# Hybrid diffusion step on one core: modulation chunks beside the long convolution, made as TensorE products instead of sums on VectorE, ScalarE and GpSimd

## The chip, the cores and the metric

The kernel runs on one core of one Trainium2 chip. The metric is the device time of one execution in microseconds (us). Engines are named as in the profile: PE is TensorE (PEld its weight loads), DVE VectorE, ACT ScalarE, POOL GpSimd, SP the queue that issues the DMAs. PE writes only to PSUM, which has eight banks of 128 partitions x 512 fp32 numbers.

## What is computed

Four layers run one after the other over 128 context tokens and 1024 latent tokens of width 1024: a long (FFT) convolution, latent attention, a recurrent mixer, and a long convolution again. Each layer begins with a modulation whose shift, scale and gate come from a condition vector, one for the latents and one for the context:

```python
def _modulation(cond, w, b):
    m = jax.nn.silu(cond) @ w + b
    return jnp.split(m, 3, axis=-1)
...
    for i in range(DEPTH):
        sh_p, sc_p, g_p = _modulation(c_ctx[None, None, :], mod_w[i], mod_b[i])
        sh_s, sc_s, g_s = _modulation(c[:, None, :], mod_w[i], mod_b[i])
        hp = xp * (1.0 + sc_p) + sh_p
        hs = xs * (1.0 + sc_s) + sh_s
...
    vf = jnp.fft.rfft(v.astype(jnp.float32), n=2 * L, axis=1)
    kf = jnp.fft.rfft(filt, axis=0)
    y = jnp.fft.irfft(vf * kf[None], n=2 * L, axis=1)[:, :L].astype(h.dtype) + v * skip
    y = y * x0
    return (y * jax.nn.silu(z)) @ w_out
```

So for each layer two vectors of 1024 are multiplied into a matrix `mod_w[i]` of 1024 x 3072. The matrix is 12 MB in fp32 and is read once for both conditions.

## The kernel before

**Modulation.** The 3072 columns are cut into six parts of 512: parts 0 and 1 are the shift, 2 and 3 the scale, 4 and 5 the gate. `mod_part` makes one part in eight steps, one for each 128 rows of the matrix (k = 0 to 7). A step loads a 128 x 512 piece (`modw`, 256 KB, two buffers) by SP at L296. DVE multiplies it by the latents' condition and adds it to `macc0` (L299 for k = 0, L302 for the rest). ACT multiplies it by the context's condition into `mprod` (L304; L300 writes `macc1` itself for k = 0), which has one buffer, and POOL adds `mprod` to `macc1` (L305). After the eighth step PE adds up the 128 partitions: for shift and scale as eight products with a column of ones, each with 128 columns of `macc` as weights (L314); for the gate as one product for each condition with the ones as weights (L326), to which DVE adds the bias (L329).

**Where the parts run.** While layer i runs, it makes its own gate (parts 4 and 5) and the next layer's shift and scale (parts 0 to 3). The first layer of all has its own shift and scale made at the start by `mod_fast`, on PE (L355). So the first layer makes six parts beside its mixer and the last one two.

**The long convolution.** Layers 0 and 3 first make the filter's spectra (`ps_ft`, `ps_sp` on PE). Then the 1024 channels go through in four units of 256 (`conv_long`). A unit transposes its signal `vx` on PE (L1073) and ACT copies it to `xt` (L1075); DVE does a first butterfly stage into `su`. Nine residues then pass through a pipeline: ACT and POOL split the fp32 numbers in two (`sh` and `sl`, L267 and L268), PE multiplies (three products each, L262 to L264, into `ps_fw`), DVE multiplies by the filter (L1108), POOL adds (L1110, L1111), ACT and POOL split again (`zh`, `zl`), PE transforms back (`ps_iv`), ACT copies out (L1137). DVE's inverse butterflies (L722 to L799) end the unit and `yc` is stored. Between these, PE does the layer's dense projections (`ps_mm<-hh,wh`, 128 x 384 each), whose results ACT copies out and DVE filters with three taps (L1006) and multiplies (L1023) into the next unit's `vx`.

**What sets the order.** The program is written as generators that `weave` interleaves by given numbers of steps: in each unit the residues, the dense jobs and 12 steps of modulation. A scheduler then sets each engine's final order. On the chip each engine runs its own list in order and waits on semaphores, and SP issues its DMAs in order. The PSUM tiles take turns through the banks that `set_banks` gives to their kind:

```python
        self.set_banks(mm=(0, 1), tp_ax_fw_iv=(2, 3, 4, 5, 6, 7))
        for q in range(NU):
            xt, xp = blocks(q, keep)
            weave((conv_long(q, keep, wpool, xt, xp), LQ[q]), (part_gen(dense, steps[q + 1]), steps[q + 1]),
                  (part_gen(rest, 12 if q < NU - 1 else 99), 12))
...
            rest = chain_gens(*(p.mod_part(*x) for x in parts))
```

Of the kernel before, what the change touches and what calls it, by code (L numbers as in the profile page):

```python
# [10 lines left out]
F32 = mybir.dt.float32  # L11
# [3 lines left out]
ALU = mybir.AluOpType  # L15
# [5 lines left out]
P = 128  # L21
D = 1024
KC = D // P
# [141 lines left out]
def weave(*jobs):  # L165

    for _ in woven(*jobs):
        pass
# [29 lines left out]
def chain_gens(*gens):  # L198
    for g in gens:
        yield from g  # L200


def part_gen(gen, steps):

    for _ in range(steps):
        try:
            next(gen)
        except StopIteration:
            return
        yield  # L210
# [12 lines left out]
class Prog:  # L223
# [66 lines left out]
    def mod_part(self, i, part):  # L290

        nc = self.nc
        acc = [self.mp.tile([P, 512], F32, tag=f"macc{c}", name=f"macc{c}", bufs=1) for c in range(2)]
        for k in range(KC):
            w = self.mp.tile([P, 512], F32, tag="modw", name="modw", bufs=2)
            nc.sync.dma_start(w, self.A["mod_w"][i, k * P:(k + 1) * P, part * 512:(part + 1) * 512])  # L296
            s, sp = self.cond[:, 0, k:k + 1], self.cond[:, 1, k:k + 1]
            if k == 0:
                nc.vector.tensor_scalar(acc[0], w, s, None, op0=ALU.mult)  # L299
                nc.scalar.activation(acc[1], w, AF.Copy, scale=sp)  # L300
            else:
                nc.vector.scalar_tensor_tensor(acc[0], w, s, acc[0], op0=ALU.mult, op1=ALU.add)  # L302
                wp = self.mp.tile([P, 512], F32, tag="mprod", name="mprod", bufs=1)
                nc.scalar.activation(wp, w, AF.Copy, scale=sp)  # L304
                nc.gpsimd.tensor_tensor(acc[1], acc[1], wp, ALU.add)  # L305
            yield
        third, half = divmod(part, 2)
        if third < 2:
            if i not in self.hsc:
                self.hsc[i] = self.cp.tile([P, 2, 2, KC], F32, tag="hsc", name=f"hsc{i}", bufs=2)  # L310
            ps = self.psum("ax")
            for c in range(2):
                for j in range(4):
                    nc.tensor.matmul(ps[:, c * 4 + j:c * 4 + j + 1], acc[c][:, j * P:(j + 1) * P],  # L314
                                     self.ones[:, 0:1], start=True, stop=True)
            for c in range(2):
                nc.vector.tensor_tensor(self.hsc[i][:, c, third, half * 4:half * 4 + 4], ps[:, c * 4:c * 4 + 4],
                                        self.vec[:, i, third, half * 4:half * 4 + 4], ALU.add)
            if third == 1 and half == 1 and i > self.first:
                self.fold_mod(i)  # L320
        else:
            if i not in self.gate:
                self.gate[i] = self.dp.tile([2, D], F32, tag="gate", name=f"gate{i}", bufs=1)
            for c in range(2):
                ps = self.psum("ax")
                nc.tensor.matmul(ps[0:1], self.ones[:, 0:1], acc[c], start=True, stop=True)  # L326
                grow = self.mp.tile([1, 512], F32, tag="mprod", name="grow", bufs=1)
                nc.sync.dma_start(grow, self.A["mod_b"][i:i + 1, part * 512:(part + 1) * 512])
                nc.vector.tensor_tensor(grow, ps[0:1], grow, ALU.add)  # L329
                nc.sync.dma_start(self.gate[i][c:c + 1, half * 512:(half + 1) * 512], grow)  # L330

    def mod_fast(self, i):

        nc = self.nc
        self.hsc[i] = self.cp.tile([P, 2, 2, KC], F32, tag="hsc", name=f"hsc{i}", bufs=2)
        rows = {}

        def channels(part):
            third, half = divmod(part, 2)
            row = rows.pop(part)  # L340
            ps = self.psum("tp")
            for j in range(4):
                nc.tensor.transpose(ps[:, 2 * j:2 * j + 2], row[:, j * P:(j + 1) * P], self.ident[:2, :2])
            for c in range(2):
                nc.vector.tensor_tensor(self.hsc[i][:, c, third, half * 4:half * 4 + 4], ps[:, c:8:2],
                                        self.vec[:, i, third, half * 4:half * 4 + 4], ALU.add)

        for part in range(4):
            acc = self.psum("mm")[:2]
            for k in range(0, KC, 2):  # L350
                w = self.wp.tile([P, 2, 512], F32, tag="wl" if k % 4 else "wh", name="modw2")
                nc.sync.dma_start(w, self.A["mod_w"][i, k * P:(k + 2) * P, part * 512:(part + 1) * 512]
                                  .rearrange("(k p) n -> p k n", p=P))
                for c in range(2):
                    nc.tensor.matmul(acc, self.cond[:, :, k + c], w[:, c], start=k + c == 0, stop=k + c == KC - 1)  # L355
                if part and k == 2:
                    channels(part - 1)
                yield
            rows[part] = self.mp.tile([2, 512], F32, tag="mprod", name="mrow", bufs=1)
            nc.vector.tensor_copy(rows[part], acc)  # L360
        channels(3)
        self.fold_mod(i)
# [606 lines left out]
    def hyena(self, i, j, lead, rest):  # L969

        nc, A, tc = self.nc, self.A, self.tc
# [189 lines left out]
        with tc.tile_pool(name="hf", bufs=1, reuse_waits="tile") as fpool:  # L1161
# [10 lines left out]
                weave((begin(), 14), (part_gen(flt, FLT), FLT))  # L1172
                steps[0] -= NG
            weave((flt, FLX - (FLT + FLA if i == self.first else 0)), (part_gen(dense, steps[0]), steps[0]))
        self.set_banks(mm=(0, 1), tp_ax_fw_iv=(2, 3, 4, 5, 6, 7))
        keep = pools.enter_context(tc.tile_pool(name="hk", bufs=1, reuse_waits="tile"))
        work = ExitStack()
        wpool = work.enter_context(tc.tile_pool(name="hl", bufs=1, reuse_waits="tile"))
# [1079 lines left out]
def build(tc, A, O, layers=(0, 1, 2, 3)):  # L2258
    with ExitStack() as ctx:
        p = Prog(ctx, tc, A, O)  # L2260
        p.setup_cond()
        first, last = layers[0], layers[-1]
        p.first = first
        lead = p.first_h()
        for i in layers:
            j = i // 3
            parts = [(i, n) for n in (4, 5)] + [(i + 1, n) for n in range(4) if i != last]
            rest = chain_gens(*(p.mod_part(*x) for x in parts))
            if i in (0, 3):
                y = p.hyena(i, j, lead, rest)  # L2270
                w_out = A["hy_w_out"][j]
            else:
                weave(lead)
                y = (p.mla if i == 1 else p.rwkv)(i, rest)
                w_out = A["mla_w_out"] if i == 1 else A["rw_w_out"]
            lead = iter(())
            p.boundary(i, w_out, y, i == last)
# [61 lines left out]
```

## Time and profile before

| what | value |
|---|---|
| time, median of 3 runs | 4587.96 us (4586.16 to 4589.27) |
| the profiled execution: its own time, its span | 4590.18 us, 4588.4 us |
| mean granted TensorE clock | 0.925 |
| PE busy | 4061.0 us (89%) |
| DVE busy | 3504.3 us (76%) |
| ACT busy | 2392.5 us (52%) |
| POOL busy | 2360.3 us (51%) |

The profile is of one execution. Busy time counts an engine's own instructions, and the rest of the span it waits. The chain of work that ended last lies for 23% on PE, 5% on DVE, 3% on DMAs and 3% on ACT. The granted clock is 1.0 for 2.4 GHz and 0.5 for 1.2 GHz. An fp32 product appears as two records on PE, so 64 records of L355 are 32 products.

### The profile page before, as it was taken

How to read it: one execution, taken by the hardware profiler on the slowest of the kernel's cores; microseconds unless marked ns; L12 is line 12 of the kernel's file. 1: busy time of each engine (PE TensorE's matmuls, PEld its weight loads, DVE VectorE, ACT ScalarE, POOL GpSimd, SP SyncE). 2: the span in 40 equal slices, each digit the busy share in tenths (PEclk: the TensorE clock that was granted, in tenths of full speed). 3: DMA queues.
4: the chain of work that ended last, by engine and by line, in shares of the span. 5: the costliest groups of instructions: out<-in, count | busy, mean ns of one | idle time of the engine just before them, and what ended most of it. 6: DMA issues, size and time to landing. Idle time of an engine off the chain costs nothing. (4 is left out here: it accounts for less than half of the span.)

```text
span 4588.4 us, 83899 instructions
## 1 busy us (share of the span) xinstructions
PE 4061.0 (89%) x30888; PEld 3510.6 (77%) x30888; DVE 3504.3 (76%) x6147; ACT 2392.5 (52%) x5468; POOL 2360.3 (51%) x1902
## 2 busy tenths in 40 slices
PE   7988988889999999879979786999999889988988
PEld 4888888678777776658867575878888678878986
DVE  7777888655998999687587997677767668967877
ACT  5554433455666666453455553666666456543331
POOL 3655766253677877455555564333333233466550
PEclk8999999999999999989988797999999899999999
DMA  5755555643000000326635464222322424665455
GB/s 169 239 181 176 164 156 157 191 149 99 19 22 21 18 28 30 121 91 203 188 108 198 145 222 136 59 79 84 83 75 68 142 93 120 214 205 153 141 155 179
DMA packets 490982, 583.04 MB, mean 127 GB/s; under 512 B 59818, under 2 KB 378332, under 8 KB 489932
## 3 DMA queue, kind: packets, MB, share of 16 engines
q1 hardware_dynamic: 489068, 576.70, 40.7%
q8 instruction: 244, 4.00, 0.4%
q14 instruction: 166, 1.36, 0.1%
q10 hardware_dynamic: 1504, 0.98, 0.1%
HBM read 413.74 MB, written 161.37 MB: 125 GB/s over the span
## 5 line engine op out<-in xcount | busy, mean ns | idle before, releaser
L262 PE MATMUL ps_mm<-hh,wh 128*128 128x384 f32 x1728 | 597.0, 347 | 47.4 <-ACT hh L267 24.0
L263 PE MATMUL ps_mm<-hl,wh 128*128 128x384 f32 x1728 | 595.6, 345 | 2.8 <-DVE hl L268 1.8
L264 PE MATMUL ps_mm<-hh,wl 128*128 128x384 f32 x1728 | 594.5, 344 | 2.7 <-POOL wl L268 2.7
L1499 POOL TENSOR_TENSOR sm<-sm,pf 128x512 f32<-128x512 f32 x288 | 443.4, 1540 | 121.8 <-ACT pf L1492 48.8
L268 POOL TENSOR_TENSOR wl<-wraw,wh 128x512 fp32r<-128x512 f32 x212 | 331.5, 1581 | 187.4 <-ACT wh L267 175.3
L262 PEld LDWEIGHTS ps_mm<-hh,wh 128*128 128x128 f32 x1728 | 335.9, 195 | 55.5 <-ACT hh L267 25.1
L1497 DVE TENSOR_TENSOR wl<-pf,wh 128x512 fp32r<-128x512 f32 x288 | 352.8, 1235 | 6.6 <-ACT wh L1493 5.8
L263 PEld LDWEIGHTS ps_mm<-hl,wh 128*128 128x128 f32 x1728 | 336.2, 195 | 7.5 <-DVE hl L268 4.4
L264 PEld LDWEIGHTS ps_mm<-hh,wl 128*128 128x128 f32 x1728 | 336.0, 194 | 6.4 <-POOL wl L268 3.8
L305 POOL TENSOR_TENSOR macc<-macc,mprod 128x512 f32<-128x512 f32 x140 | 211.8, 1513 | 178.0 <-ACT mprod L304 155.4
L263 PE MATMUL ps_mm<-mx,wh 128*128 128x384 f32 x680 | 253.6, 373 | 37.9 <-DVE mx L1669 36.9
L262 PE MATMUL ps_mm<-mx,wh 128*128 128x384 f32 x680 | 255.9, 378 | 19.9 <-ACT mx L1668 6.1
L262 PE MATMUL ps_mm<-woh,hh 128*128 128x512 f32 x576 | 233.8, 407 | 37.0 <-ACT hh L267 34.6
L2144 POOL TENSOR_TENSOR tot<-SV,wcs 64x128 f32<-64x128 f32 x288 | 115.6, 405 | 267.9 <-DVE SV L2172 245.2
L264 PE MATMUL ps_mm<-mx,wl 128*128 128x384 f32 x680 | 247.0, 364 | 3.1 <-POOL wl L268 3.1
L1492 ACT ACTIVATE pf<-ps_st 128x512 f32<-128x512 f32 x288 | 172.3, 598 | 144.9 <-POOL sm L1499 53.3
L264 PE MATMUL ps_mm<-woh,hl 128*128 128x512 f32 x576 | 234.1, 406 | 3.7 <-DVE hl L268 3.7
L302 DVE SCALAR_TENSOR_TENSOR macc<-modw,cond,macc 128x512 f32<-128x512 f32 x140 | 156.5, 1118 | 103.3 <-DMA modw<-mod_w 102.4
L1437 DVE TENSOR_REDUCE mx<-ps_pj 128x1 f32<-128x512 f32 (+2 forms) x400 | 220.4, 575 | 17.2 <-PE ps_pj L1436 16.4
L263 PE MATMUL ps_mm<-wol,hh 128*128 128x512 f32 x576 | 231.8, 402 | 0.0
L304 ACT ACTIVATE mprod<-modw,cond 128x512 f32<-128x512 f32 x140 | 101.3, 723 | 205.5 <-POOL macc L305 108.6
L1493 ACT ACTIVATE wh<-ps_st 128x512 fp32r<-128x512 f32 x336 | 194.3, 578 | 0.0
(560 smaller groups left out, 13149.2 us busy)
## 6 DMA issues: line engine op xcount, KB each, us to landing
cst<-cst SPq DMA_DIRECT2D x175, 384.0 KB
modw<-mod_w SPq DMA_DIRECT2D x160, 256.0 KB
wraw<-hy_w_in SPq DMA_DIRECT2D x128, 256.0 KB
kd<-kt SPq DMA_DIRECT2D x72, 384.0 KB
kt<-kd SPq DMA_DIRECT2D x72, 384.0 KB
cst<-cst SPq DMA_DIRECT2D x41, 512.0 KB
ctd<-ct SPq DMA_DIRECT2D x24, 768.0 KB
bkd<-bk SPq DMA_DIRECT2D x24, 768.0 KB
```

The source lines that it names most:

```text
L262: mm(ps, lh, rh, start=start, stop=False)
L263: mm(ps, lh, rl, start=False, stop=False)
L264: mm(ps, ll, rh, start=False, stop=stop)
L268: (lo_eng or self.nc.gpsimd).tensor_tensor(lo, src, hi, ALU.subtract)
L302: nc.vector.scalar_tensor_tensor(acc[0], w, s, acc[0], op0=ALU.mult, op1=ALU.add)
L305: nc.gpsimd.tensor_tensor(acc[1], acc[1], wp, ALU.add)
L1437: nc.vector.tensor_reduce(mx[:, t, j:j + 1], ps, AX.X, ALU.max)
L1492: nc.scalar.activation(pf, s, AF.Exp, scale=scale)
L1493: nc.scalar.activation(ph, s, AF.Exp, scale=scale)
L1497: nc.vector.tensor_tensor(pl, pf, ph, ALU.subtract)
L1499: nc.gpsimd.tensor_tensor(sm, sm, pf, ALU.add)
L2144: g_.tensor_tensor(tot[h], SV[e][h, jsl], wc[h].unsqueeze(2).broadcast_to([64, 2, 64]), M)
```

## The change

In layers 0 and 3 the parts are made by a new generator `mod_rows`. Both conditions, as a 128 x 2 weight, are multiplied with each 128 x 512 piece on PE, and the eight products add up in one bank, in fp32. That bank (7) is taken from the group for transposes, residues and inverse, which is left with five. After the eighth product DVE copies the two rows out, PE transposes four pieces of 2 x 128, and DVE adds the bias for shift and scale; for the gate DVE adds the bias to the two rows and one DMA stores both. `mod_part` stays for layers 1 and 2.

```diff
+    def mod_rows(self, i, part):
+
+        nc, cols = self.nc, slice(part * 512, (part + 1) * 512)
+        acc = self.psum("md")[:2]
+        for k in range(KC):
+            w = self.mp.tile([P, 512], F32, tag="modw", name="modw", bufs=2)
+            nc.sync.dma_start(w, self.A["mod_w"][i, k * P:(k + 1) * P, cols])
+            nc.tensor.matmul(acc, self.cond[:, :, k], w, start=k == 0, stop=k == KC - 1)
+            yield
+        third, half = divmod(part, 2)
+        row = self.mp.tile([2, 512], F32, tag="mprod", name="mrow", bufs=1)
+        if third < 2:
...
+            nc.vector.tensor_copy(row, acc)
+            ps = self.psum("ax")
+            for j in range(4):
+                nc.tensor.transpose(ps[:, 2 * j:2 * j + 2], row[:, j * P:(j + 1) * P], self.ident[:2, :2])
+            for c in range(2):
+                nc.vector.tensor_tensor(self.hsc[i][:, c, third, half * 4:half * 4 + 4], ps[:, c:8:2],
+                                        self.vec[:, i, third, half * 4:half * 4 + 4], ALU.add)
...
+        else:
...
+            nc.sync.dma_start(row, self.A["mod_b"][i, cols].partition_broadcast(2))
+            nc.vector.tensor_tensor(row, acc, row, ALU.add)
+            nc.sync.dma_start(self.gate[i][:, half * 512:(half + 1) * 512], row)
...
-        self.set_banks(mm=(0, 1), tp_ax_fw_iv=(2, 3, 4, 5, 6, 7))
+        self.set_banks(mm=(0, 1), tp_ax_fw_iv=(2, 3, 4, 5, 6), md=(7,))
...
-            rest = chain_gens(*(p.mod_part(*x) for x in parts))
+            rest = chain_gens(*((p.mod_rows if i in (0, 3) else p.mod_part)(*x) for x in parts))
```

The added function moves all later lines by 30 (L1073 becomes L1103). In the new kernel L338 is the load of `modw`, L339 the product, L346 and L359 what DVE does with the two rows, L349 the transposes.

The scheduler's order changes with it. First PE in layer 0, where the first unit ends and the signal of the second is transposed (`ps_tp`). Before:

```order
L262 MATMUL ps_mm<-hh,wh 128x384
L263 MATMUL ps_mm<-hl,wh 128x384
L264 MATMUL ps_mm<-hh,wl 128x384
L1073 MATMUL ps_tp<-ident,vx 128x128 x13
L262 MATMUL ps_fw<-sh,cst 128x256
L263 MATMUL ps_fw<-sl,cst 128x256
```

and after the change:

```order
L262 MATMUL ps_mm<-hh,wh 128x384
L263 MATMUL ps_mm<-hl,wh 128x384
L264 MATMUL ps_mm<-hh,wl 128x384
L1103 MATMUL ps_tp<-ident,vx 128x128 x13
L339 MATMUL ps_md<-modw,cond 2x512 x2
L262 MATMUL ps_fw<-sh,cst 128x256
```

The products (`ps_md`) stand in PE's own list between its other work. Of the 48 in layer 0, six pairs follow one another directly and 36 stand alone; of the 16 in layer 3, three pairs and ten alone. From the last inverse product of the first unit to these 13 transposes the list has 120 dense products before, and 140 and five modulation products after.

Next DVE at the same place, up to the end of `vx`, for which the transposes wait. Before:

```order
L1006 SCALAR_TENSOR_TENSOR xx<-up,cw,xx 128x1153
L784 SCALAR_TENSOR_TENSOR st<-st 128x256
L785 SCALAR_TENSOR_TENSOR st<-st 128x256
L787 TENSOR_TENSOR st<-su 128x256
L788 TENSOR_TENSOR st<-su 128x256
L302 SCALAR_TENSOR_TENSOR macc_4531<-modw,cond,macc_4531 128x512
L1006 SCALAR_TENSOR_TENSOR xx<-up,cw,xx 128x1153
L791 SCALAR_TENSOR_TENSOR st<-st 128x256
L792 SCALAR_TENSOR_TENSOR st<-st 128x256
L302 SCALAR_TENSOR_TENSOR macc_4531<-modw,cond,macc_4531 128x512
L1023 TENSOR_TENSOR vx<-vx,xx 128x1153
```

and after the change:

```order
L826 TENSOR_TENSOR st<-st 128x256
L829 TENSOR_TENSOR st<-st 128x256
L784 SCALAR_TENSOR_TENSOR yc<-st,yc 128x2x128 x2
L826 TENSOR_TENSOR st<-st 128x256
L829 TENSOR_TENSOR st<-st 128x256
L784 SCALAR_TENSOR_TENSOR yc<-st,yc 128x2x128 x2
L1036 SCALAR_TENSOR_TENSOR xx<-up,cw,xx 128x1153 x2
L1053 TENSOR_TENSOR vx<-vx,xx 128x1153
```

The sums into `macc` are gone from the list, and `vx` now ends behind the last eight inverse butterflies, which stood behind it before.

Last POOL at the same place. Before:

```order
L1111 TENSOR_TENSOR m<-m 128x256
L268 TENSOR_TENSOR zl<-m,zh 128x512
L268 TENSOR_TENSOR wl<-wraw,wh 128x512 x2
L305 TENSOR_TENSOR macc_4532<-macc_4532,mprod 128x512 x3
L268 TENSOR_TENSOR wl<-wraw,wh 128x512 x2
L305 TENSOR_TENSOR macc_4532<-macc_4532,mprod 128x512 x4
L268 TENSOR_TENSOR sl<-xp,sh 128x256
```

and after the change:

```order
L1141 TENSOR_TENSOR m<-m 128x256
L268 TENSOR_TENSOR zl<-m,zh 128x512
L268 TENSOR_TENSOR wl<-wraw,wh 128x512 x4
L268 TENSOR_TENSOR sl<-xp,sh 128x256
L1140 TENSOR_TENSOR m<-m 128x256
```

The seven sums are gone, and POOL has only splits left between two units.

## Rows read from the trace of the kernel before

**Rows 1.** Stretches: length, PE/PEld/DVE/ACT/POOL busy (instructions), PE clock, DMA share, GB/s.

```profile
355.00:800.00 445.00, 390.56 (x2382) 378.96 (x2381) 361.83 (x582) 180.22 (x353) 293.48 (x221) 0.94 0.53 164
...
4110.00:4470.00 360.00, 325.74 (x2012) 315.30 (x2010) 273.96 (x498) 136.40 (x276) 211.03 (x161) 0.96 0.50 154
```

**Rows 2.** Waits of PE from 290 to 800 us: in total, times, longest.

```profile
PE ps_tp L1073 <- DVE up L992: 12.4, 1, 12.4
PE ps_mm L262 <- ACT xx L1000: 9.8, 2, 5.7
...
PE ps_sp L262 <- DMA cst<-cst: 5.2, 2, 5.0
...
PE ps_sp L262 <- ACT fsh L267: 4.0, 1, 4.0
```

**Rows 3.** Waits of PE from 3990 to 4470 us: the longest.

```profile
PE ps_tp L1073 <- DVE up L992: 11.8, 1, 11.8
```

**Rows 4.** Modulation by line, 290 to 860 us: busy, mean ns, idle before, releasers.

```profile
L305 POOL TENSOR_TENSOR macc<-macc,mprod 128x512 f32<-128x512 f32 x42 | 68.4, 1628 | 46.1 <-ACT mprod L304 36.9 <-ACT macc L300 6.8 <-PE ps_fw L264 2.5
...
L302 DVE SCALAR_TENSOR_TENSOR macc<-modw,cond,macc 128x512 f32<-128x512 f32 x42 | 44.7, 1065 | 10.5 <-DMA modw<-mod_w 10.4
...
L304 ACT ACTIVATE mprod<-modw,cond 128x512 f32<-128x512 f32 x42 | 30.5, 726 | 75.4 <-POOL macc L305 37.3 <-DMA modw<-mod_w 35.5 <-DVE macc L302 1.8
```

**Rows 5.** DVE by line, 425.3 to 461.2 us: the sums into macc.

```profile
L302 DVE SCALAR_TENSOR_TENSOR macc<-modw,cond,macc 128x512 f32<-128x512 f32 x7 | 6.1, 872 | 0.0
```

**Rows 6.** DVE in order of time from 446 us: start, us, instruction.

```profile
447.07 1.52 DVE L768 TENSOR_TENSOR st<-st 128x256 f32<-128x256 f32 x1
448.51 0.41 DVE L772 TENSOR_TENSOR st<-st 128x256 f32<-128x256 f32 x1
```

**Rows 7.** POOL in order of time, the same 4 us.

```profile
446.71 1.59 POOL L305 TENSOR_TENSOR macc<-macc,mprod 128x512 f32<-128x512 f32 x1 [0.84 <-ACT mprod L304]
```

**Rows 8.** ACT in order of time: modulation's products at 309 and 581 us.

```profile
308.79 0.72 ACT L304 ACTIVATE mprod<-modw,cond 128x512 f32<-128x512 f32 x1 [5.91 <-POOL macc L305]
...
581.42 0.72 ACT L304 ACTIVATE mprod<-modw,cond 128x512 f32<-128x512 f32 x1 [5.67 <-DMA modw<-mod_w]
```

**Rows 9.** SP's DMA issues in order of time, 324 to 332 us.

```profile
324.62 0.42 SPq L953 DMA_DIRECT2D kd<-kt  x1
330.65 0.33 SPq L296 DMA_DIRECT2D modw<-mod_w  x1
...
331.42 0.53 SPq L634 DMA_DIRECT2D cst<-cst  x1
```

**Rows 10.** Stretches at half clock behind these waits: one of six, and their sum.

```profile
452.10:465.80 13.70, 4.47 (x21) 4.47 (x22) 12.50 (x26) 2.74 (x5) 3.06 (x3) 0.50 0.21 68
...
sum 51.20, PE 26.81 PEld 26.85 DVE 39.53 ACT 15.14 POOL 18.42; mean PE 4.47 PEld 4.47 DVE 6.59 ACT 2.52 POOL 3.07
```

**Rows 11.** PE in order of time: one fp32 product alone between dense products.

```profile
4116.81 0.33 PE L263 MATMUL ps_mm<-hl,wh 128*128 128x384 f32 x1
4116.99 0.34 PE L264 MATMUL ps_mm<-hh,wl 128*128 128x384 f32 x1
4117.26 1.02 PE L326 MATMUL ps_ax<-macc,ones 128*1 128x512 f32 x2
...
4118.49 0.34 PE L263 MATMUL ps_mm<-hl,wh 128*128 128x384 f32 x1
```

**Rows 12.** PE in order of time: transposes, an fp32 pair, eight with ones.

```profile
50.16 0.40 PE L343 MATMUL ps_tp<-ident,mrow 2*128 2x2 f32 x4
...
424.23 1.88 PE L326 MATMUL ps_ax<-macc,ones 128*1 128x512 f32 x4
...
557.20 1.84 PE L314 MATMUL ps_ax<-ones,macc 128*128 128x1 f32 x16
```

**Rows 13.** A load of modw issued by SP, and ACT waiting for it.

```profile
447.23 0.33 SPq L296 DMA_DIRECT2D modw<-mod_w  x1
...
450.24 0.72 ACT L304 ACTIVATE mprod<-modw,cond 128x512 f32<-128x512 f32 x1 [3.61 <-DMA modw<-mod_w]
```

More of the change, by code (lines that the diff above doesn't have):

```diff
@@ L330, in mod_part @@
                 nc.sync.dma_start(self.gate[i][c:c + 1, half * 512:(half + 1) * 512], grow)
+    def mod_rows(self, i, part):
[9 more added lines that the diff above has]
+        if third < 2:
+            if i not in self.hsc:
+                self.hsc[i] = self.cp.tile([P, 2, 2, KC], F32, tag="hsc", name=f"hsc{i}", bufs=2)
+            nc.vector.tensor_copy(row, acc)
[5 more added lines that the diff above has]
+                                        self.vec[:, i, third, half * 4:half * 4 + 4], ALU.add)
+            if third == 1 and half == 1 and i > self.first:
+                self.fold_mod(i)
+        else:
+            if i not in self.gate:
+                self.gate[i] = self.dp.tile([2, D], F32, tag="gate", name=f"gate{i}", bufs=1)
+            nc.sync.dma_start(row, self.A["mod_b"][i, cols].partition_broadcast(2))
+            nc.vector.tensor_tensor(row, acc, row, ALU.add)
+            nc.sync.dma_start(self.gate[i][:, half * 512:(half + 1) * 512], row)
     def mod_fast(self, i):
```

## The prediction

> **What bounds the kernel now.** I read the page's busy shares first: PE 89%, DVE 76%, ACT and POOL about half. PE is nearest to the bound, but the share is a mean over the whole span, so the second view is that of stretches. The four units of the convolution are 355 to 800 us in layer 0 and 4110 to 4470 us in layer 3 [rows 1]. PE is busy for 390.56 of 445.00 us and 325.74 of 360.00 us: it waits 54.4 and 34.3 us. DVE, at 361.83 and 273.96 us, is second. So in these stages the end is set by PE's list plus what PE waits; work added to PE costs its own length unless it stands where PE would have waited, and work taken from the others pays only by a PE wait that ends.
>
> The third view is therefore that of PE's waits [rows 2, 3]. The longest of each layer, 12.4 and 11.8 us, is that of the transposes for `vx`, which DVE finishes. Then come 9.8 us for `xx`, which ACT begins, 5.0 us of the 5.2 for a load of `cst`, and 4.0 us for ACT's split of the filter. Now who made those late:
>
> - The 12.4 and 11.8: in the 36 us before 461 us DVE makes seven of the sums, 6.1 us [rows 5], and POOL makes its seven in the same time. A butterfly that runs beside a POOL sum takes 1.52 us, the next one without it 0.41 [rows 6, 7], so each POOL sum costs DVE about 1.1 us too. Sums and stretching together are up to 6.1 + 7 x 1.1 = 13.8 us of DVE, as much as the wait.
> - The 4.0 and 9.8: ACT stands in its list at a modulation product, 5.91 us for POOL's sum and 5.67 us for a load of `modw` [rows 8], and what PE needs is queued behind it. Over 290 to 860 us ACT waits so for 37.3 us (POOL) and 35.5 us (loads) [rows 4].
> - The 5.0: SP issues nothing between 324.62 and 330.65 us, where the `modw` load waits for its buffer; the load of `cst` goes out behind it at 331.42 [rows 9].
>
> Behind each such wait PE's clock is at 0.50. Six stretches hold 26.81 us of PE work at that clock [rows 10]; at 1.0 it would be half of that, so 13.4 us are lost.
>
> **The change part by part.** *Removed.* Of the sums on DVE, ACT and POOL, 44.7, 30.5 and 68.4 us of busy time in layer 0 alone [rows 4], nothing counts directly, since PE is the bound. What counts is the waits they cause: 12.4 + 9.8 + 5.0 + 4.0 + 11.8 = 43.0 us, and 13.4 us of clock, in all 56.4 us. From PE itself go 8 products with ones on the gates: the pair takes 1.88 us [rows 12], one alone adds 1.14: from 4116.99 to 4118.49 us stand it and one dense product, so 1.50 less two pitches of 0.18 [rows 11]. Half of each kind: 4 x 0.94 + 4 x 1.14 = 8.3 us. And four groups of eight for the next layer at 1.84 [rows 12]: 7.4 us.
>
> *Added.* 64 fp32 products of 512 columns. The order has 46 alone and 18 in pairs: 46 x 1.14 + 18 x 0.94 = 69.4 us. I take the row alone for the singles, since they too stand between dense products. Four times four transposes, 0.40 each [rows 12]: 1.6 us. DVE's copies and additions are few and lie under PE. So PE's list grows by 69.4 + 1.6 - 8.3 - 7.4 = 55.3 us.
>
> What the row shows of a product is 0.94 us back to back and 1.14 alone. The Trainium skill ("FP8 and Floating Point Precision", section "TensorE Precision Notes") says that true fp32 takes four passes through the array; an estimate by it, 4 x 512 columns at 2.4 GHz, is 0.85 us, so 54.6 us for 64 and a sum lower by some 15 us. No row here reaches it, so I stay with the rows.
>
> *Moved.* `vx` of the second unit now ends behind eight inverse butterflies: 8 x 0.41 = 3.3 us later on DVE [rows 6], against the 13.8 us saved there. PE's transposes stand behind 140 dense and five modulation products in place of 120: 20 x 0.18 + 5 x 1.14 = 9.3 us of work in front of them. Both speak for the 12.4 us wait going entirely.
>
> *Loads.* The same 64 loads go out, but each now frees its buffer when PE has multiplied it, and PE waits for each. A load takes 3.0 us from issue to use (447.23 to 450.24 us) [rows 13], and with two buffers and some 9 us between products (410 us for 48) it is there in time as a rule. Bounds: nothing if always; if PE waits as ACT did, 35.5 us [rows 4] for layer 0 and a third of it, 11.8, for layer 3, in all 47.3 us. I take two landings, 6 us, near the lower end, since ACT's waits came much from a buffer held by the slowest of three readers, and now there is one.
>
> *Banks.* The transposes, residues and inverse take turns in five banks in place of six, and a part's first product waits until DVE has read the one before. Lower bound nothing. Upper bound: one wait like the 4.0 us of [rows 2] in each of the eight units, 32 us. The large waits of before are for data, none for a bank; I take nothing.
>
> *The other waits.* After the 43.0 us there remain 54.4 - 22.2 = 32.2 us (layer 0 without its 12.4 and 9.8) and 34.3 - 11.8 = 22.5 us, in all 54.7 [rows 1 to 3]: splits of ACT and POOL, loads of `cst`. DVE, ACT and POOL are freer, and PE arrives later, so some go. Bounds: none, or all of it. I take a quarter, 14 us, since the loads of `cst` and the chains through a residue stay as they are.
>
> *Sum.* +55.3 - 56.4 + 6 - 14 = -9.1 us, against the profiled execution's 4590.18 us (its span is 4588.4): 4581.1. That run was 2.2 us above the median, 4587.96; so against the median 4579 us.
>
> **The rivals.**
>
> *B, PE becomes the bound of the stage.* Of the remaining 54.7 us a half to two thirds (27 to 36) goes, since most of them end with an engine that the change relieves, and no load is late: 55.3 - 56.4 - 27 to 36 = -28 to -37, in the middle 4556 us. For it: POOL loses 68.4 us of sums in layer 0, and its splits are what several of the remaining waits end with. Against: a relieved engine lets the scheduler's list run tighter, but a residue's chain of split, product, multiplication, split stays as long.
>
> *C, slower: PE waits for the loads in its own list.* An in-order engine stands still for a `modw` piece as ACT did. Place: the 64 products; price: up to 47.3 us, and half clock behind the longer ones, for which 10 us is my guess (nearly the 13.4 of now). -9 + 47 - 6 + 10 = +42, 4630 us. With 6 us already in the sum, it decides from new waits of 6 + 9 = 15 us on (no gain) and from 24 us on a measurable loss. For it: the loads share SP's list with `cst`, `wraw` and the stores, and SP's wait for a buffer now lasts until PE gets to the product. Against: loads have 9 us for 3.0.
>
> *D, the waits come back in other clothes.* PE's product waits are set by several things; of the 56.4 us only about half (28) returns, because behind `vx` the next residue's load or split is late. -9 + 28 = +19, 4607 us. For it: PE's idle time is spread over many small waits; the named ones are those that ended last. Against: the long ones have one cause each, seen in the rows.
>
> *E, one product costs less.* If all 64 take 0.94, the added work is 60.2 in place of 69.4 us: 9 less, 4570 us.
>
> By the four passes of the Trainium skill's section on TensorE precision it would be an estimated 4564 us; in these rows the product in pairs is 0.94, so that rule alone does not give the time here.
>
> **How the numbers follow.** Chances: my forecast 0.42, with its own range 4566 to 4594 (a few us on each term); B 0.20; C 0.15; D 0.18; E 0.05. The predicted time is the likeliest, 4579 us. The range should leave 0.2 out: below, the far end of B, above, most of C. I take 4542 to 4617: down to 4542 for the part of B where nearly all of the 54.7 us goes, up to 4617 to hold D and the smaller half of C. About 0.2% of the time, 9.2 us, is what a measurement can tell from no change. My forecast's -9 lies on that bound: half of it, 0.21, counts as faster and 0.19 as the same, 0.02 as slower; B and E are faster (0.25); D is same for 0.08 and slower for 0.10; C is slower for nearly all, 0.14, and 0.01 same. Faster 0.46, same 0.28, slower 0.26.
>
> **What would show it.** Right: the wait of `ps_tp` for `up` is gone from both layers, those for `xx` and `fsh` too; granted clock in the two stretches above 0.94 and 0.96 [rows 1]; PE busy over the kernel up by about 42 us (55.3 - 13.4 of clock); the products at 1.02 us each; DVE's butterflies at 0.41. Wrong: waits of PE at L339 for `modw` above 15 us (C); equal idle time in the stretches under other names (D); a product that adds clearly more or less than 1.14 us; waits of the first product of a residue for a bank's reader. Most likely to make me wrong is the size of the other waits: a quarter of 54.7 is a choice, and each tenth of it is 5 us.

## The result and the profile after

The changed kernel takes 4532.28 us (median of 4 runs, 4524.27 to 4535.43), the kernel before 4587.06 us beside it: a ratio of 0.9879, 95% interval [0.9862, 0.9896]. It is faster by about 55 us, where 9 were forecast, and lies below the range. The profiled execution took 4535.43 us. Two executions in a slower state, one of the kernel before (5212.53 us) and one of x_fours, its profiled one (9183.00 us), count in none of the ratios below.

The page's head after the change:

```profile
span 4533.6 us, 83746 instructions
...
PE 4085.7 (90%) x30952; PEld 3478.1 (77%) x30952; DVE 3388.5 (75%) x6083; ACT 2349.1 (52%) x5404; POOL 2258.6 (50%) x1846
...
PEclk8999999988999999989978697999999799999999
```

PE is busy for 25 us more and the kernel is 55 us shorter. The stretch of layer 0 that [rows 1] show before, over the same times after (its columns as there):

```profile
355.00:800.00 445.00, 425.30 (x2459) 368.75 (x2458) 304.99 (x573) 157.93 (x316) 236.22 (x187) 0.98 0.59 183
```

PE waits 19.7 of these 445 us, where it waited 54.4, and the clock is at 0.98 in place of 0.94. Waits of PE from 290 to 800 us after:

```profile
PE ps_fw L262 <- DMA cst<-cst: 5.0, 4, 1.6
PE ps_mm L262 <- ACT woh L267: 4.2, 1, 4.2
PE ps_fw L263 <- POOL sl L268: 2.6, 3, 1.4
PE ps_sp L262 <- DMA cst<-cst: 2.3, 2, 1.7
...
PE ps_mm L262 <- ACT xx L1030: 1.3, 1, 1.3
...
PE ps_md L339 <- DVE mrow L359: 0.7, 1, 0.7
```

Of [rows 2] the 12.4 us for `up` and the 4.0 for `fsh` are gone, the 9.8 for `xx` are 1.3, the 5.2 of `ps_sp` for `cst` are 2.3. No wait for `modw` is in this list. At the place of the 12.4 us PE now runs like this, in order of time:

```profile
440.08 1.02 PE L339 MATMUL ps_md<-modw,cond 128*2 128x512 f32 x2
...
445.30 1.58 PE L1103 MATMUL ps_tp<-ident,vx 128*128 128x128 f32 x13
```

The transposes begin with no wait, after dense work that goes on until then. The wait of [rows 3] is gone as well. For `modw` PE waits in layer 3 alone, from 3930 to 4420 us:

```profile
PE ps_md L339 <- DMA modw<-mod_w: 0.5, 2, 0.4
```

All products of layer 0, by line:

```profile
L339 PE MATMUL ps_md<-modw,cond 128*2 128x512 f32 x96 | 48.0, 592 | 0.7 <-DVE mrow L359 0.7
```

**Where the 55 us came from.** Layer times before and after don't fall on the same microseconds, so I cut both traces at the same instructions: layer 0 from one fixed product of the filter's spectra to the first product of layer 1's attention, layer 3 from one such product to the last inverse product. Before:

```profile
301.80:1081.40 779.60, 677.09 (x3831) 631.52 (x3830) 558.61 (x922) 343.21 (x688) 426.51 (x300) 0.93 0.51 158
4008.50:4435.00 426.50, 373.54 (x2319) 361.19 (x2319) 310.41 (x550) 165.46 (x334) 265.96 (x202) 0.94 0.53 164
```

and after:

```profile
301.70:1043.10 741.40, 696.27 (x3871) 608.75 (x3870) 471.53 (x874) 313.42 (x643) 352.83 (x259) 0.97 0.54 166
3979.70:4381.40 401.70, 375.90 (x2348) 351.87 (x2347) 289.05 (x531) 156.68 (x321) 235.34 (x188) 0.99 0.56 175
```

Together they are 63.0 us shorter (38.2 and 24.8); the rest of the program, which the change leaves alone, was some 8 us longer in this execution. To see what the 63 are made of, take all stretches of the two pieces in which the granted clock is 0.50, 24 before and 9 after. Their sums, before:

```profile
sum 156.70, PE 104.83 PEld 96.59 DVE 104.00 ACT 51.26 POOL 80.17; mean PE 4.37 PEld 4.02 DVE 4.33 ACT 2.14 POOL 3.34
```

and after:

```profile
sum 47.90, PE 35.23 PEld 28.01 DVE 21.41 ACT 17.89 POOL 22.25; mean PE 3.91 PEld 3.11 DVE 2.38 ACT 1.99 POOL 2.47
```

Half of PE's busy time there is lost by the clock: 52.4 us before, 17.6 after. Length less busy is what PE waits: 155.5 before, 70.9 after. What is left is PE's work at full clock: 998 before, 1055 after. So -85 of waits, -35 of clock, +56 of work make the -63.

### The profile page after: what moved, and what is told of

It reads as the page before. It is cut to its first block, busy times and chain, and to the rows that moved or that the text cites. A ratio compares the mean times of both kernels' runs of the same rounds, so it can differ in the third digit from the quotient of the medians.

```text
span 4533.6 us, 83746 instructions
## 1 busy us (share of the span) xinstructions
PE 4085.7 (90%) x30952; PEld 3478.1 (77%) x30952; DVE 3388.5 (75%) x6083; ACT 2349.1 (52%) x5404; POOL 2258.6 (50%) x1846
## 5 line engine op out<-in xcount | busy, mean ns | idle before, releaser
L264 PE MATMUL ps_mm<-hh,wl 128*128 128x384 f32 x1728 | 585.2, 339 | 0.0
L267 ACT CAST wh<-wraw 128x512 fp32r<-128x512 f32 x212 | 122.2, 617 | 147.2 <-PE ps_mm L263 84.2
L580 POOL TENSOR_TENSOR s<-s,ln_rows 128x1024 f32<-128x1024 f32 x36 | 95.5, 2653 | 187.9 <-PE ps_tp L443 155.0
L1497 PE MATMUL ps_pv<-wl,vv 128*128 128x512 f32 x336 | 148.5, 442 | 37.5 <-DVE wl L1527 35.2
```

The costliest lines, as they stand in the source:

```text
L264: mm(ps, ll, rh, start=False, stop=stop)
L267: self.nc.scalar.copy(hi, src)
L1497: nc.tensor.matmul(pv, vl, pl, start=False, stop=last)
```

## The experiments

The table cuts each kernel's trace at the same instructions and splits the two pieces in that way (waits: length less PE busy; lost: half of PE's busy time at 0.50; work: the rest). Time against before is the ratio applied to 4587 us, so 0.1% is 4.6 us. The pieces are of one profiled execution each, and executions of one kernel lie up to 41 us apart, so a few us between two pieces say little.

Each edit lets the scheduler order the program anew. Even x_bank, which has the instructions of the kernel before, has another order on DVE, and no run holds the order still. So a difference of some 10 us can be the order's. The 55 us are hardly that: six kernels with the whole relief and an order of their own on DVE (the changed one, x_short, x_pairs, x_fours, x_noload, x_short_noload) lie between 4524 and 4532 us.

| kernel | ratio to before [95%] | us against before | two pieces | work | waits | lost |
|---|---|---|---|---|---|---|
| before | 1 | 0 | 1206 | 998 | 155 | 52 |
| changed | 0.9879 [0.9862, 0.9896] | -55 | 1143 | 1055 | 71 | 18 |
| x_short | 0.9878 [0.9856, 0.9900] | -56 | 1147 | 1007 | 103 | 36 |
| x_both | 1.0042 [1.0026, 1.0059] | +19 | 1231 | 1066 | 118 | 47 |
| x_half2 | 0.9956 [0.9939, 0.9973] | -20 | 1174 | 1068 | 82 | 24 |
| x_double | 0.9999 [0.9984, 1.0015] | 0 | 1187 | 1091 | 78 | 17 |
| x_noctx | 0.9918 [0.9904, 0.9932] | -38 | 1163 | 998 | 119 | 46 |
| x_nosum | 0.9914 [0.9895, 0.9933] | -39 | 1161 | 997 | 114 | 51 |
| x_nolat | 0.9977 [0.9968, 0.9986] | -11 | 1184 | 1000 | 137 | 47 |
| x_bank | 1.0023 [1.0008, 1.0038] | +11 | 1208 | 999 | 154 | 55 |
| x_pairs | 0.9883 [0.9865, 0.9902] | -54 | 1149 | 1050 | 80 | 19 |

**Is the gain relief, or cover?** Two theories: the other engines are freer, so that what PE waits for comes sooner (relief); or PE's own added work lies where it would have waited (cover). Two kernels tell them apart. x_short has the relief without the work:

```diff
-            nc.tensor.matmul(acc, self.cond[:, :, k], w, start=k == 0, stop=k == KC - 1)
+            n = 512 if k == 0 else 8
+            nc.tensor.matmul(acc[:, :n], self.cond[:, :, k], w[:, :n], start=k == 0, stop=k == KC - 1)
```

> The changed kernel, but of the eight products of a part seven take only the first 8 of 512 columns (the outputs lack the rest); all 64 loads, the order of parts and the relief of DVE, ACT and POOL stay. 56 products of about 1 us go from PE. Theory 1 (relief): the waits of PE ended because the other engines are freer. Then they do not come back without the products, and the time falls from 4532 us by most of 56 x 1.0, to 4475 to 4490. Theory 2 (cover): the waits only lie under the added work, since PE comes later. Then they come back and the time falls by less than 20 us, to 4515 or more.

It took 4529.19 us (4509.86 to 4537.36), the same as the changed kernel: 56 products cut to almost nothing save nothing. Its two pieces:

```profile
302.30:1039.90 737.60, 672.31 (x3871) 617.56 (x3871) 480.52 (x874) 313.65 (x643) 372.27 (x259) 0.95 0.53 167
3973.60:4382.90 409.30, 371.41 (x2346) 359.16 (x2346) 295.72 (x530) 156.26 (x320) 235.01 (x188) 0.96 0.55 172
```

PE is busy 28 us less than in the changed kernel and the pieces are 4 us longer. The work that went (47 us at full clock) came back as 32 us of waits and 19 of lost clock. Waits of PE from 355 to 800 us in x_short:

```profile
PE ps_fw L262 <- DMA cst<-cst: 10.4, 5, 4.0
PE ps_iv L262 <- ACT zh L267: 8.4, 3, 7.3
PE ps_md L340 <- DMA modw<-mod_w: 4.5, 2, 3.7
```

So cover holds for the price of the work; and relief for the gain, since with 9 us of added work in place of 56 the time falls by the same 56 us.

x_both is the other half, the work without the relief:

```diff
+        md = self.psum("md")[:2] if "md" in self.banks else None
         for k in range(KC):
...
+            if md is not None:
+                nc.tensor.matmul(md, self.cond[:, :, k], w, start=k == 0, stop=k == KC - 1)
...
-        self.set_banks(mm=(0, 1), tp_ax_fw_iv=(2, 3, 4, 5, 6, 7))
+        self.set_banks(mm=(0, 1), tp_ax_fw_iv=(2, 3, 4, 5, 6), md=(7,))
```

> The kernel before with all its sums on DVE, ACT and POOL, and beside them the 64 products on PE into a bank of their own (their result is not used). PE's list grows by about 64 to 69 us, nothing is relieved. Theory 1 (relief): the waits of before stay, so the time is 4587 + 55 to 75 = 4640 to 4660. Theory 2 (cover): a good part of the added work falls into the old waits, so 4590 to 4615.

4602.47 us (4594.28 to 4607.43), as cover had it. 68 us of work make the pieces 25 us longer, the time 19. x_both also takes bank 7 from its group, as x_bank does below, so part of the 19 can be the bank's. PE was not the bound before either.

**How far does cover go?** x_double issues each product of the changed kernel twice, x_half2 every second one:

```diff
-            nc.tensor.matmul(acc, self.cond[:, :, k], w, start=k == 0, stop=k == KC - 1)
+            for n in range(2):
+                nc.tensor.matmul(acc, self.cond[:, :, k], w, start=k + n == 0, stop=k + n == KC)
```

```diff
-            nc.tensor.matmul(acc, self.cond[:, :, k], w, start=k == 0, stop=k == KC - 1)
+            for n in range(1 + k % 2):
+                nc.tensor.matmul(acc, self.cond[:, :, k], w, start=k == 0, stop=k + n == KC)
```

> The changed kernel with each of the 64 products issued twice (the outputs get twice the modulation product): PE's list grows by another 64 to 70 us, the other engines as in the changed kernel. In the two convolution layers 71 us of waits and 18 us of lost clock are left, of which some lie behind the convolution. If the added work of the change was covered by waits of PE and half of what is left can cover more: 4532 + 25 to 45 = 4557 to 4577. If PE is now the bound: 4532 + 60 to 70 = 4592 to 4602. If cover is as good as it was for the first 64: under 4545.

> The changed kernel with every second product issued twice (32 more on PE, some 32 us; the outputs get a different modulation product). Cutting 56 products of the changed kernel cost and gained nothing, doubling all 64 cost 46 to 55 us. If PE is the bound from the changed kernel's amount of work on: 4532 + 20 to 30 = 4552 to 4562. If there is still cover for a half: 4532 to 4545, and the next 32 would carry the whole cost.

They took 4578.73 us (4570.09 to 4591.82) and 4562.37 us (4558.28 to 4570.76). Layer 0 in x_half2, and then in x_double:

```profile
301.00:1056.90 755.90, 713.89 (x3919) 611.78 (x3919) 470.39 (x874) 313.46 (x643) 336.58 (x259) 0.98 0.53 163
```

```profile
303.70:1075.10 771.40, 731.57 (x3968) 613.35 (x3967) 471.88 (x874) 313.38 (x643) 348.04 (x259) 0.98 0.52 160
```

From 741.4 us it grows by 14.5 and 30.0, for 19 and 40 us of work: three quarters of the length, where the first 34 us (x_short to the changed kernel) added 3.8. In layer 3 both kernels are longer too, by 17 and 14 us, though there the two pieces hold less work than in the changed kernel: 80 and 96 of the dense products stand behind the last unit in their order. By the time of the whole kernel the further 32 and 64 products cost 35 and 55 us (the table's -20 and 0 against -55), which is about their whole length at 0.84 to 1.10 us each. So the knee lies near the changed kernel's amount of work. x_half2 came out at the upper end of my case with PE as the bound; x_double lies between two of its cases, half cover and PE as the bound.

**Which relief?** x_noctx leaves out ACT's products and POOL's sums in the two layers, x_nosum POOL's sums alone, x_nolat DVE's sums alone; nothing is added to PE. In this order:

```diff
+        conv = i == 0 or (i == 1 and part < 4) or i == 3 and part > 3
...
-                nc.scalar.activation(acc[1], w, AF.Copy, scale=sp)
+                if not conv:
+                    nc.scalar.activation(acc[1], w, AF.Copy, scale=sp)
...
+                if conv:
+                    yield
+                    continue
                 wp = self.mp.tile([P, 512], F32, tag="mprod", name="mprod", bufs=1)
```

```diff
+        conv = i == 0 or (i == 1 and part < 4) or i == 3 and part > 3
...
-                nc.gpsimd.tensor_tensor(acc[1], acc[1], wp, ALU.add)
+                if not conv:
+                    nc.gpsimd.tensor_tensor(acc[1], acc[1], wp, ALU.add)
```

```diff
+        conv = i == 0 or (i == 1 and part < 4) or i == 3 and part > 3
...
-                nc.vector.scalar_tensor_tensor(acc[0], w, s, acc[0], op0=ALU.mult, op1=ALU.add)
+                if not conv:
+                    nc.vector.scalar_tensor_tensor(acc[0], w, s, acc[0], op0=ALU.mult, op1=ALU.add)
```

> The kernel before without the context's half in the two layers: no products on ACT, no sums on POOL (the context gets the latents' modulation there); DVE's sums and all loads stay, nothing is added to PE. Cutting the products short in the changed kernel gave 4529 us, about 55 below before, which is the whole relief. Theory P (ACT's list and POOL's sums, which also stretch DVE): 4535 to 4548. Theory D (DVE's own 45 us of sums a layer): 4568 or more.

> The kernel before without POOL's sums of the context alone in the two layers (ACT's products stay and are thrown away, so the context's modulation holds its first product only); DVE's sums and all loads stay. Leaving out ACT's and POOL's share together gave 4543. If POOL's sums are what counts (ACT's products wait for them, DVE is stretched by them): 4543 to 4555. If ACT's products in their list, waiting for loads, count: 4565 or more.

> The other half: the kernel before without the latents' sums on DVE in the two layers (the latents get the context's modulation there); ACT's products, POOL's sums and all loads stay, nothing is added to PE. Theory P: little, 4565 to 4587. Theory D: most of the relief, 4530 to 4548. If either half alone is enough to end the waits, both kernels are at 4545 or below.

4543.11, 4542.72 and 4569.92 us. POOL's sums alone carry 39 of the 56 us; leaving out ACT's products beside them adds nothing that can be told, and DVE's own sums are worth 11. Leaving out POOL's sums ends three things at once: their time on POOL, ACT's waits for `mprod`'s one buffer, and what they cost DVE; no run separates the three. The two pieces of x_nosum:

```profile
302.00:1043.10 741.10, 672.77 (x3830) 627.67 (x3829) 515.24 (x921) 340.79 (x686) 360.04 (x259) 0.95 0.54 166
3962.40:4382.60 420.20, 374.63 (x2319) 362.22 (x2319) 307.39 (x550) 164.80 (x333) 245.17 (x188) 0.94 0.54 166
```

In layer 0 DVE has one instruction less than before (921 and 922) and is busy for 515.24 us in place of 558.61. The 41 sums that POOL no longer makes there (259 instructions in place of 300) cost DVE 43.4 us, 1.06 us each, as [rows 6] had suggested with 1.1. In layer 3 that doesn't hold: 14 sums less, and DVE is busy for 307.39 us in place of 310.41, 0.2 us each. The piece gains 38.5 us in layer 0 and 6.3 in layer 3.

**The bank.** x_bank is the kernel before with five banks in the group and the eighth unused:

```diff
-        self.set_banks(mm=(0, 1), tp_ax_fw_iv=(2, 3, 4, 5, 6, 7))
+        self.set_banks(mm=(0, 1), tp_ax_fw_iv=(2, 3, 4, 5, 6))
```

> The kernel before, with bank 7 taken from the transposes, residues and inverses of the convolution and used by nobody. If the sixth bank was not needed, as the forecast took it: 4587 us within 9. If each unit waits once for a bank: 4600 to 4620. A gain (another order of the lists) would have to show as fewer waits of PE.

4588.85 us (4576.85 to 4608.01) against 4581.04 beside it: 4 to 17 us slower by the interval. Its profile puts only 2 of these into the two pieces. I took nothing; it may be a few us.

**The price and the loads.** x_pairs issues the products two at a time, x_fours four at a time with two more buffers. x_noload loads one piece for a part in place of eight and multiplies it eight times; x_short_noload does that with the products cut. The edits of x_pairs and x_noload:

```diff
-            nc.tensor.matmul(acc, self.cond[:, :, k], w, start=k == 0, stop=k == KC - 1)
+            ws = ws + [w] if k % 2 else [w]
+            for n, w in enumerate(ws if k % 2 else ()):
+                nc.tensor.matmul(acc, self.cond[:, :, k - 1 + n], w, start=k + n == 1, stop=k + n == KC)
```

```diff
-            w = self.mp.tile([P, 512], F32, tag="modw", name="modw", bufs=2)
-            nc.sync.dma_start(w, self.A["mod_w"][i, k * P:(k + 1) * P, cols])
+            if k == 0:
+                w = self.mp.tile([P, 512], F32, tag="modw", name="modw", bufs=2)
+                nc.sync.dma_start(w, self.A["mod_w"][i, k * P:(k + 1) * P, cols])
```

> The changed kernel with the products issued two at a time, after both loads, with the same two buffers: 23 pairs and 18 alone in PE's list, where there were 9 and 46. If a product alone costs 0.2 us more than one in a pair, 28 x 0.2 = 5.6 us are saved: 4526 us. If the buffers, now held two at a time, make PE wait for loads: 4540 and more, with waits for modw in the list of waits.

> The changed kernel with four loads and then four products (two more buffers, from the sums that are gone): ten fours in PE's list, the rest shorter. If the price of a product mattered, 4532 - 8 to 12. Since the work of PE in these layers is mostly covered, I expect the same time as the changed kernel within 9 us; four loads at once on SP's queue could cost up to 10 us where loads of cst stand behind them.

> The changed kernel with all 64 full products but one load of modw a part. The changed kernel shows 0.5 us of PE waiting for modw, so by the waits the loads cost nothing: 4532 within 9. If loads of cst come earlier without them: 4515 to 4523.

> The changed kernel with the products cut to 8 columns in seven of eight, and one load of modw a part in place of eight (56 of 64 loads left out, the outputs use one piece for all). If the loads on SP's queue set the pace of the stages with the products cut short: 4500 to 4520, with fewer waits for cst. If the chains through splits, butterflies and copies set it: 4525 to 4535, as with all loads.

4527.87, 4530.74, 4524.18 and 4525.49 us; ratios 0.9883, 0.9886 [0.9870, 0.9902], 0.9877 [0.9849, 0.9906] and 0.9875 [0.9850, 0.9900]. All are the changed kernel's time, within 9 us for the first two and some 13 for the others. In x_pairs PE has 5 us less work, as the price of a product alone had it, and the time doesn't show it: savings of 6 to 12 us can't be told here. Nor do 56 of the 64 loads cost anything that can be told. In x_short_noload the two pieces are 15 us shorter than in x_short, but these are two profiled executions 17 us apart (4520.64 and 4537.36), while the medians are 4 apart. If the loads of `modw` set the pace, it is by less than the interval.

**The other layers.** x_rw makes the products on PE in layer 2 too, x_all in layers 1 and 2:

```diff
-        self.set_banks(mm_tp_ax=tuple(range(8)))
+        self.set_banks(mm_tp_ax=tuple(range(7)), md=(7,))
...
-            rest = chain_gens(*((p.mod_rows if i in (0, 3) else p.mod_part)(*x) for x in parts))
+            rest = chain_gens(*((p.mod_rows if i in (0, 2, 3) else p.mod_part)(*x) for x in parts))
```

> The changed kernel with the products on PE in layer 2 (the recurrent mixer) too, bank 7 taken there from the eight that all kinds share. PE waits and half clock in layers 1 and 2 come to about 300 and 185 us, so by the two effects (other engines relieved, added work covered) the 48 products should cost nothing and some waits should end: 4500 to 4530. If that stage waits for something that the modulation does not touch, 4532 within 9; if the bank was needed, more.

> The products on PE in all four layers (in layer 1 bank 5 is theirs and the transposes share 3 and 4). By relief and cover: the gain of layer 2 as in the kernel with three layers, and the like for layer 1, 4480 to 4520. If layer 1's dense part is bound by PE: 4532 + 40.

4531.57 us, ratio 0.9884 [0.9865, 0.9903], and 4540.19 us, 0.9903 [0.9885, 0.9922]. Neither is better than the changed kernel, and my expectation of a gain was wrong for both. In x_all PE does wait for the loads, from 1039 to 3978 us:

```profile
PE ps_md L339 <- DMA modw<-mod_w: 13.4, 12, 4.1
```

No kernel tried beats the changed one.

## Why the prediction was wrong

- **PE's list grows by 55.3 us**: right as work. 56.4 us were measured, 1.10 us a product after the other terms. Cutting 504 of 512 columns took 47.3 us from 56 products, 0.84 each. The Trainium skill ("FP8 and Floating Point Precision", section "TensorE Precision Notes") says that true fp32 takes four passes through the array; an estimate by it, 4 x 504 columns at 2.4 GHz, is 0.84 us, and the measured 0.84 agrees. The other 0.26 of the 1.10 us stay with a product of 8 columns in x_short.
- **The step that failed** is what this work costs in time. I wrote that "work added to PE costs its own length unless it stands where PE would have waited", and then gave the cover only "a quarter, 14 us" of the other waits, relief and cover in one term. Relief and cover add up. Relief alone makes the two pieces 59 us shorter (x_short), with 9 us of work added, so 68 of waits and clock went: the sum had 43.0 + 13.4 + 14 - 6 = 64. Then 47 us of work take away another 51 of waits and clock, which the sum didn't have. In all 84.6 us of waits went where the sum had 43.0 + 14 - 6 = 51, and 34.8 of clock where it had 13.4. I read a stage with PE at 88 to 90% as bound by PE. It was not: x_both shows that 68 us of work cost it 25.
- **Waits removed, 43.0 us**: nearly right. Those for `up` are gone in both layers, that for `fsh` too; between 290 and 800 us those for `xx` are 1.3 us and those of `ps_sp` for `cst` 2.3. POOL's sums stand behind most of the relief (x_nosum: 39 of 56 us); ACT's waits for loads of `modw` were not worth anything that x_noctx and x_nosum can tell apart. The Trainium skill ("SBUF — State Buffer", section "Who interferes with whom") says that a DVE instruction with two SBUF inputs contends with a GpSimd instruction that reads SBUF. The 1.06 us of DVE for each POOL sum in layer 0 agree with it; the 0.2 in layer 3 show that it is no fixed price of a sum.
- **The clock, 13.4 us**: 34.8 measured. I counted the six stretches behind the waits that I had named, out of 24. So PE's busy time over the kernel rose by 25 us, where I had 42.
- **The other waits, a quarter of 54.7**: of 84.6 us that went in all, some 42 are not among the named. The list of 54.7 stopped at 800 us; the wait of 12.5 us at 821 us for `hh`, behind the last unit, is 4.2 (for `woh`) in the changed kernel.
- **Loads, 6 us**: 0.5 us in the waits, all in layer 3, and nothing that can be told in the time (x_noload). Rival C did not happen.
- **Moved, and banks**: the transposes found `vx` ready, as forecast. For the bank I took nothing; x_bank is 4 to 17 us slower, of which its pieces show 2.
- **The rivals**: nearest was B, by its sign and its cause, but it too charged all of PE's work and stopped at -37. D did not happen: of 155 us of waits 71 are left. E's cheaper product showed as 5 us of PE's work in x_pairs and not in the time.

What sets the pace of the two stages when PE has room stays open. It is not PE's work (x_short), nor, within the intervals, the loads of `modw`; POOL's sums were part of it. The waits left in x_short name loads of `cst` and the splits on ACT, and no run separates these.

## What to carry to other kernels

A busy share near 90% does not make an engine the bound: if its waits are many and short, ask what the added work would lie under, and test it by adding the work alone and by taking it away alone. Here 47 us of PE work were free (x_short against the changed kernel), and 32 or 64 products more cost about their whole length. Where an engine waits in many places, count what one other engine's instruction does to all that share its path, not only the longest waits: POOL's sums took POOL's time, held ACT at its next product and stretched DVE in layer 0, and leaving out these sums alone gave 39 us. And a stage's waits do not end where its main loop does.

## What was not expected of the hardware

The clock follows the waits more closely than I had counted: 24 stretches at 0.50 in the two pieces before, 9 after, so 35 of the 63 us that the two pieces gained are PE time that half clock no longer takes. And work that keeps PE running pays part of its price by that: of the 51 us that 47 us of products took away from x_short, 19 are clock.
